# Dilated units later in the pipeline, a rope in pairs of rows, and wide value matmuls in a two-layer encoder

## Chip, cores, metric

The kernel runs on one core of one Trainium2 chip. The metric is the device time of one execution in microseconds. Five engines work side by side: TensorE (PE, with its weight loads shown as PEld), VectorE (DVE), ScalarE (ACT), GpSimd (POOL) and SyncE (SP, which issues DMAs). Each works off its own list of instructions in order, and they wait for one another by semaphores.

## What is computed

A two-layer encoder on 256 tokens of width 1024, in float32. Each layer projects the normalised input to three attention mixers and to gates, adds the gated mixers, and ends with a SwiGLU block:

```
for l in range(DEPTH):
    h = rms_norm(x, g_mix[l]); proj = h @ w_in[l]
    c_q, c_kv, k_r, qkv_b, qkv_c, gate_logits = split(proj)
    y_a = mla_mixer(c_q, c_kv, k_r, ...)                       # 8 heads
    q_b = apply_rope(qkv_b[:, :, 0], cos_b, sin_b)             # 12 heads of 64
    k_b = apply_rope(qkv_b[:, :, 1], cos_b, sin_b)
    y_b = dilated_mixer(q_b, k_b, qkv_b[:, :, 2])              # 3 dilations x 4 heads
    y_c = neighbourhood_mixer(*qkv_c, rpb[l])                  # 8 heads
    gates = sigmoid(gate_logits)
    x = x + (gates[0]*(y_a @ w_pa) + gates[1]*(y_b @ w_pb) + gates[2]*(y_c @ w_pc)) @ w_o[l]
    h = rms_norm(x, g_ffn[l])
    x = x + (silu(h @ w1[l]) * (h @ w3[l])) @ w2[l]
```

`apply_rope` splits a head's 64 rows into two halves x1 and x2 and returns x1 cos - x2 sin and x2 cos + x1 sin, so that row i needs row i + 32 of its head.

## The kernel before

**Split products.** Every large product is made of three matmuls in a rounded type (fp32r): weights and activations are each split into a high and a low part, and high x high, high x low and low x high are added in PSUM (`mm3`, and `v_mm` where the tokens are stationary and the weights move). Weights come as chunks of 128 x 1024 float32 in a fixed order (`PLAN`, made by `plan`), by DMAs on SP's queue into `raw` (6 buffers). ACT casts a chunk to `hi` (L292) and DVE subtracts to `lo` (L294), 4 buffers each. `take` hands out the next chunk and has the one after it split. `pack_weights` lays the chunks out on the host.

**Units.** Attention is cut into units of one half of the queries: 8 of kind c (neighbourhood, a head pair each), 8 of kind a (latent, a head pair each), 8 of kind b (dilated, one head of each of the three groups). A unit passes a pipeline of slots: in a slot's end the newest unit gets its scores (PE), the one before it is transposed (PE, `ps_t`) and copied (ACT), and the one before that is multiplied with V (PE, `ps_y`). In a slot's begin DVE normalises p (L510, L513) ahead of the transposes. `add_units` puts units into the list `todo`; each `slot_end` takes one. Slots stand in the code between the weight tiles: 6 around the dilated q tiles, 6 around the dilated values, 6 around the dilated k tiles, then one behind each of the 24 gate tiles. The units of kind c and a fill the first 16 slots and leave the pipeline in the next two, so the units of kind b, added behind the last k tile, enter with gate tile 0.

**Rope.** `b_tiles` makes the 6 q (or k) tiles in 3 pairs. Behind a pair ACT copies the PSUM bank to t0 (L858), four DMAs on ACT's own queue (L860) exchange blocks of 32 partitions into t1, and DVE multiplies the bank with the cosines into t2 (L861). `rope_end`, called in the middle of the next pair and behind the last, has POOL multiply t1 with the sines (L834) and add (L836 to QB or KB, L839 for the first pair, which then goes through `stack` with two DMAs on POOL's queue). t0, t1, t2 and other scratch share one tag, `t2k`, with 4 buffers in rotation. A dilated unit's scores are two 256-column products with Q0 and K0 and, for each of the other two dilations, two 64x64 products with QB and KB (each shown as two PE records): the first dilation's take the middle pair of tiles, the second's the last pair.

**Values.** Three value tiles of 256 columns (`v_tile`), each with two chunks of 512 weight rows, 48 matmuls, into one PSUM bank of tag g (2 banks in rotation, shared with the q, k and gate tiles). Behind each stand two slots. Tile 0 is evicted by two ACT operations (L696), tile 1 by four on 64 partitions (L880), tile 2 by two and two DMAs (L885).

**What sets the order.** The code gives priorities, and a scheduler that simulates the engines while the kernel is built puts each engine's instructions in a fixed order: an instruction is placed when its inputs are ready in that simulation. So PE's list has matmuls of the next tile in between a unit's steps.

The lines that the change touches are `consts`, `plan`, `pack_weights`, and in `encoder` L859 (DMAs of the rope), L870 to L887 (values), L892 (`add_units` of kind b) and L903 to L905 (the gate loop).

Of the kernel before, what the change touches and what calls it, by code (L numbers as in the profile page):

```python
# [10 lines left out]
F32 = mybir.dt.float32  # L11
# [12 lines left out]
EPS = 1e-6  # L24
BIG = 1e30
HD = 64
OFF_B = 416
OFF_C = OFF_B + 3 * 12 * HD
OFF_G = OFF_C + 3 * 8 * HD
# [8 lines left out]
def consts():  # L38


    def rope(dim):
        pos = np.arange(S, dtype=np.float32)
        inv = np.power(np.float32(10000.0), -np.arange(0, dim, 2, dtype=np.float32) / np.float32(dim))
        ang = pos[:, None] * inv[None, :].astype(np.float32)
        return np.cos(ang).astype(np.float32), np.sin(ang).astype(np.float32)

    f = np.float32
    parts = {}
    rows = np.arange(P)
    parts["ident"] = np.eye(P, dtype=f)  # L50
    parts["ones"] = np.ones((P, P), f)
    parts["col"] = np.tile(np.array([1 / 1024, 1 / 256, 1 / 128, EPS], f), (P, 1))
    c, s = rope(32)
    r = np.arange(32)
    cs = c[TOK][:, r % 16].T
    sn = (s[TOK][:, r % 16] * np.where(r < 16, -1.0, 1.0)[None, :]).T
    sc = f(MLA_SCALE)
    for name, v in (("ck", cs), ("sk", sn)):
        parts[name] = v.T.reshape(2, P, 32).transpose(1, 0, 2).reshape(P, 64)

    parts["tm"] = np.concatenate([np.tile(v, (4, 1)) * sc for v in (cs, np.roll(sn, 16, 0))], 1)
    t = TOK


    dm = np.zeros((P, 2, 384), f)
    for h in range(2):
        q = t[h * P : (h + 1) * P][:, None]
        k = t[None, :]
        dm[:, h, 0:256] = np.where(np.abs(q - k) <= 64, 0, -8 * BIG)
        for e in range(2):  # L70
            r = slice(64 * e, 64 * e + 64)
            dm[r, h, 320 - 64 * e : 384 - 64 * e] = np.where((q[r] - q[r].T) % 16 == 0, 0, -8 * BIG)
    c, s = rope(HD)
    d = rows % 64
    parts["cosb"] = c[TOK][:, d % 32].T
    parts["sinb"] = (s[TOK][:, d % 32] * np.where(d < 32, -1.0, 1.0)[None, :]).T
    parts["dmask"] = dm.reshape(P, -1)
    at, col = {}, 0
    for k, v in parts.items():
        at[k] = (col, v.shape[1])  # L80
        col += v.shape[1]
    return np.ascontiguousarray(np.concatenate(list(parts.values()), 1).astype(f)), at
# [12 lines left out]
def plan():  # L95

    out = [(("a", k), 640) for k in range(KC)]
    out += [(("ck", i), 1024) for i in (2, 3)] + [(("cq", i), 1024) for i in range(4)]
    out += [(("uq", 0), 768)] + [(("cv", 0, h), 1024) for h in range(2)] + [(("uq", 1), 768)]
    for k, n in LAST:  # L100
        out += [(("cvk", k, n), 288 * n)] + [(("ukv",), 1024)] * (k == 0)
    out += [(("b", "q", i), 1024) for i in range(6)]
    out += [(("bv", i, h), 1024) for i in range(3) for h in range(2)]
    out += [(("b", "k", i), 1024) for i in range(6)]
    out += [(("g", j, br), 1024) for j in range(8) for br in range(3)]
    for j in range(10):
        if j < 8:
            out += [(("mab", j), 768), (("mc", j), 512)]
        if j > 1:
            out += [(("o", j - 2), 1024)]  # L110
    out += [(("f", c), 1024) for c in range(4)]
    for f in range(2, NF):
        out += [(("w1", f), 1024), (("w3", f), 1024)]
        if f > 2:
            out += [(("w2", f - 3), 1024)]
    out += [(("w2", f), 1024) for f in range(NF - 3, NF)]
    return out
# [6 lines left out]
def pack_weights(i, l):  # L124
# [17 lines left out]
    def part(key):  # L142
        n = key[0]
        if n == "a":
            c = np.concatenate([np.arange(384), nb_heads("ck", 0), nb_heads("ck", 1)])
            return w_in[P * key[1] : P * key[1] + P, c]
        if n in ("ck", "cq"):
            return tiles(w_in, nb_heads(n, key[1]))
        if n == "cvk":
            c = np.concatenate([OFF_C + 1280 + np.arange(256), 384 + n32])  # L150
            return tiles(w_in[P * key[1] : P * (key[1] + key[2])], c)
        if n in ("cv", "bv"):
            base = OFF_C + 1024 if n == "cv" else OFF_B + 1536
            return tiles(w_in[512 * key[2] : 512 * key[2] + 512], base + 256 * key[1] + np.arange(256))
        if n == "uq":

            cols = [h * 96 + n64 for h in range(4 * key[1], 4 * key[1] + 4)]
            cols += [h * 96 + 64 + n32 for h in range(key[1], 8, 2)]
            return tiles(w_uq, np.concatenate(cols))
        if n == "ukv":  # L160
            ks = np.concatenate([h * P + n64 for h in range(8)])
            return tiles(w_ukv, np.concatenate([ks, ks + 64]))
        if n == "b":
            base = OFF_B + (0 if key[1] == "q" else 768)
            t = key[2]
            return tiles(w_in, heads(base, (2 * t, 2 * t + 1)))
        if n == "g":
            return tiles(w_in, OFF_G + key[2] * D + key[1] * P + np.arange(P))
        cols = np.arange(key[1] * P, key[1] * P + P)
        if n == "mab":  # L170
            return np.concatenate([tiles(i["w_pa"][l], cols), tiles(i["w_pb"][l], cols)], 1)
        if n == "mc":
            return tiles(i["w_pc"][l], cols)
        if n == "o":
            return i["w_o"][l][cols]
        if n == "w2":
            return i["w2"][l][cols]
        if n == "f":
            k = slice(256 * key[1], 256 * key[1] + 256)
            return np.concatenate(  # L180
                [
                    np.concatenate([i[w][l][k][c * P : c * P + P, f * P : f * P + P] for f in (0, 1) for w in ("w1", "w3")], 1)
                    for c in range(2)
                ],
                1,
            )
        return tiles(i[n][l], cols)
# [45 lines left out]
def encoder(ctx: ExitStack, tc: tile.TileContext, x, w, gains, cst, rpb, gfin, out):  # L233
# [375 lines left out]
    if True:  # L609
# [33 lines left out]
        for l in range(NL):  # L643
# [201 lines left out]
            def b_tiles(w_, dst):  # L845
                for i2 in range(3):
                    o = bank("g", "ps_g")
                    for i in range(2):
                        slot_begin()
                        n_tile(l, o[:, cols(i, S)], ("b", w_, 2 * i2 + i))  # L850
                        if i == 0:
                            rope_end()
                        if i == 1:
                            o3 = o.rearrange("p (n s) -> p n s", n=2)
                            t0 = tmp.tile([P, 512], F32, tag="t2k", name="t0", bufs=4)
                            t1 = tmp.tile([P, 512], F32, tag="t2k", name="t1", bufs=4)
                            t2 = tmp.tile([P, 2, S], F32, tag="t2k", name="t2", bufs=4)
                            act.copy(t0, o)  # L858
                            for q in range(4):  # L859
                                act.dma_start(t1[cols(q, 32)], t0[cols(q ^ 1, 32)])  # L860
                            dve.tensor_mul(t2, o3, bc(CR, 2))  # L861
                        slot_end()
                    rope.append((t1.rearrange("p (n s) -> p n s", n=2), t2, dst, w_, i2))
# [3 lines left out]
            K0 = tmp.tile([P, 2, 4, S], F32R, tag="ks", name="K0", bufs=1)  # L867
            KL = [K0[:, e, 2:4, :] for e in range(2)]
            other_rows(KL)
            for i in range(3):  # L870
                o = bank("g", "ps_g")
                slot_begin()
                v_tile(o, "bv", i)
                rope_end()
                if i == 0:
                    v_out(VB, o, 0, RT)
                elif i == 1:
                    for b in range(4):
                        r, t = cols(b % 2, 64), b // 2
                        act.activation(VB[r, 2 + b, :], o[r, cols(t, S)], AF.Copy, scale=RT[r, t : t + 1])  # L880
                else:
                    v2 = tmp.tile([P, 2, 256], F32, tag="t2k", name="v2", bufs=4)
                    v_out(v2, o, 0, RT)
                    for b in range(2):
                        act.dma_start(VB[cols(1 - b, 64), 2 + b :: 2, :], v2[cols(b, 64)])  # L885
                slot_end()
                slot_begin()  # L887
                slot_end()
            KB = tmp.tile([P, 4, S], F32, tag="kb", name="KB", bufs=1)
            b_tiles("k", KB)  # L890
            rope_end()
            add_units(  # L892
                "b", 4, Q=QB, K=KB, V=VB, V12=VB[:, 2:6, :], Q0=[Q0[:, e] for e in range(2)], K0=[K0[:, e] for e in range(2)], L=KL
            )


            GL0 = tmp.tile([P, 16, S], F32, tag="big", name="GL0", bufs=1)
            GL1 = [tmp.tile([P, 4, S], F32, tag=t, name="GL1", bufs=b) for t, b in (("u4a", 2), ("u4a", 2), ("v4", 1))]
# [4 lines left out]
            for i2 in range(12):  # L903
                o = bank("g", "ps_g")
                for i in range(2):  # L905
                    slot_begin()
                    n = 2 * i2 + i
                    n_tile(l, o[:, cols(i, S)], ("g", n // 3, n % 3))
                    if i == 1:
                        (d0, n0), (d1, n1) = logits(n - 1), logits(n)  # L910
# [210 lines left out]
```

## Time and profile before

| | us |
|---|---|
| median of 3 runs (923.6 to 926.31) | 926.07 |
| the profiled execution | 925.92 |
| its span, first to last instruction | 924.1 |
| PE busy | 906.0 |
| DVE busy | 660.8 |
| ACT busy | 519.1 |
| POOL busy | 128.9 |

The granted TensorE clock was 0.997 of full speed over the span. Busy time of PE is a sum over modelled ends: a 256-column matmul is shown with 0.28 us though the next one starts 0.12 later, so the starts tell the pace and a gap between starts tells a wait. A wait's idle time, in square brackets in a row, counts from the shown end.

The stretch that the change touches runs, in layer 0, from about 62 us (first dilated q tile) over 81 (values) and 109 (k tiles) to about 205 (last gate tile), and in layer 1 some 453 us later.

### The profile page before, as it was taken

The page shows a single profiled execution, that of the slowest core. Times are in us where ns is not written, and L with a number is a line of the kernel's source. Part 1 is how long each engine was busy: PE and PEld are TensorE (multiplying, and loading weights), DVE is VectorE, ACT ScalarE, POOL GpSimd, SP SyncE. Part 2 cuts the span into 40 slices and gives each one's busy share as a digit, 9 for nine tenths or more (in the row PEclk, how much of TensorE's full clock was granted, in tenths as well). Part 3 has the DMA queues.
Part 4 walks back from the last instruction along what each step waited for, and adds up shares of the span by engine and source line. Part 5 has one row for each costly group of instructions (what it writes and reads, how often), then busy time and mean ns, then how long its engine had stood idle before and what let it go on. Part 6 is the DMA issues. An engine that isn't in the chain of part 4 may idle for free. (4 is left out here: it accounts for less than half of the span.)

```text
span 924.1 us, 18598 instructions
## 1 busy us (share of the span) xinstructions
PE 906.0 (98%) x7446; PEld 871.0 (94%) x7446; DVE 660.8 (72%) x1003; ACT 519.1 (56%) x858; POOL 128.9 (14%) x138
## 2 busy tenths in 40 slices
PE   8999999999999999999999999999999999999996
PEld 6999898999999999999999989899999999999995
DVE  6987877555888766666699888665577976666663
ACT  6776875533566544444477778655355654444443
POOL 2223112000022100000023240400000210000000
PEclk9999999999999999999999999999999999999998
DMA  8985455344675766655467644533457566555531
GB/s 290 286 289 174 133 149 150 107 153 148 193 223 183 258 209 195 184 185 184 119 237 213 211 147 135 173 117 124 145 178 214 168 212 205 184 193 184 195 124 45
DMA packets 53414, 166.71 MB, mean 180 GB/s; under 512 B 6736, under 2 KB 7504, under 8 KB 53328
## 3 DMA queue, kind: packets, MB, share of 16 engines
q1 hardware_dynamic: 48384, 158.69, 53.7%
q0 software_dynamic: 1920, 3.15, 1.6%
q10 hardware_dynamic: 3024, 3.69, 1.5%
q8 instruction: 58, 0.95, 0.4%
q14 instruction: 28, 0.23, 0.1%
HBM read 157.64 MB, written 1.05 MB: 172 GB/s over the span
## 5 line engine op out<-in xcount | busy, mean ns | idle before, releaser
L294 DVE TENSOR_TENSOR lo<-raw,hi 128x1024 fp32r<-128x1024 f32 (+4 forms) x306 | 373.3, 1227 | 153.4 <-ACT hi L292 152.1
L292 ACT CAST hi<-raw 128x1024 fp32r<-128x1024 f32 (+5 forms) x308 | 304.1, 992 | 301.8 <-PE ps_g L318 162.7
L318 PE MATMUL ps_g<-XH,hi 128*128 128x256 f32 x1392 | 390.0, 281 | 1.2 <-ACT hi L292 1.2
L318 PE MATMUL ps_g<-XH,lo 128*128 128x256 f32 x1392 | 387.9, 281 | 1.6 <-DVE lo L294 1.6
L318 PE MATMUL ps_g<-XL,hi 128*128 128x256 f32 x1392 | 389.3, 280 | 0.0
L318 PEld LDWEIGHTS ps_g<-XH,hi 128*128 128x128 f32 x1392 | 261.5, 188 | 5.2 <-issue 1.9
L318 PEld LDWEIGHTS ps_g<-XH,lo 128*128 128x128 f32 x1392 | 260.2, 188 | 5.3 <-issue 2.7
L318 PEld LDWEIGHTS ps_g<-XL,hi 128*128 128x128 f32 x1392 | 261.7, 188 | 1.6 <-issue 0.3
L318 PE MATMUL ps_acc<-HL,hi 128*128 128x256 f32 x608 | 109.3, 279 | 0.0
L318 PEld LDWEIGHTS ps_acc<-HL,hi 128*128 128x128 f32 x608 | 93.1, 188 | 0.0
L318 PE MATMUL ps_acc<-HL,lo 128*128 128x256 f32 x304 | 84.2, 280 | 0.0
L995 POOL TENSOR_TENSOR SG<-fab 128x256 f32<-128x256 f32 x44 | 34.5, 786 | 305.7 <-DVE fab L991 302.5
L318 PEld LDWEIGHTS ps_acc<-HL,lo 128*128 128x128 f32 x304 | 57.1, 188 | 0.0
L318 PE MATMUL ps_acc<-hi,HL 128*128 128x512 f32 x176 | 55.3, 395 | 0.0
L318 PE MATMUL ps_g<-hi,XL 128*128 128x256 f32 (+1 forms) x160 | 45.9, 287 | 0.0
L318 PE MATMUL ps_g<-hi,XH 128*128 128x256 f32 (+1 forms) x160 | 45.4, 284 | 0.0
L318 PE MATMUL ps_g<-lo,XH 128*128 128x256 f32 (+1 forms) x160 | 45.2, 285 | 0.0
L991 DVE TENSOR_TENSOR fab<-ps_g,RB 128x512 f32<-128x512 f32 x40 | 27.6, 691 | 21.9 <-PE ps_g L318 21.9
L528 ACT COPY pT<-ps_t 128x512 f32<-128x512 f32 (+1 forms) x48 | 26.0, 551 | 29.0 <-PE ps_t L518 21.8
L318 PEld LDWEIGHTS ps_acc<-hi,HL 128*128 128x128 f32 x176 | 31.7, 188 | 6.1
L318 PE MATMUL ps_acc<-lo,HL 128*128 128x512 f32 x88 | 34.8, 395 | 0.0
L834 POOL TENSOR_TENSOR t<-t,CSR 128x512 f32<-128x512 f32 x12 | 19.7, 1644 | 107.9 <-DMA t<-t 79.1
(194 smaller groups left out, 1263.0 us busy)
## 6 DMA issues: line engine op xcount, KB each, us to landing
raw<-in_w SPq DMA_DIRECT2D x250, 512.0 KB, 3.6
raw<-in_w SPq DMA_DIRECT2D x20, 384.0 KB, 3.1
raw<-in_w SPq DMA_DIRECT2D x16, 320.0 KB, 3.1
braw<-in_rpb SPq DMA_DIRECT2D x16, 256.0 KB, 5.2
raw<-in_w SPq DMA_DIRECT2D x16, 256.0 KB, 2.7
t<-t ACTq DMA_DIRECT2D x48, 64.0 KB, 4.4
raw<-in_w SPq DMA_DIRECT2D x4, 432.0 KB, 4.9
KCt<-KCt POOLq DMA_DIRECT2D x8, 128.0 KB, 5.8
```

What stands on the lines that cost most here:

```text
L292: act.copy(hi[:, :width], t[:, :width])
L294: ins = eng.tensor_sub(lo[:, :width], t[:, :width], f32(hi[:, :width])).ins
L318: pe.matmul(o, a, b, start=start, stop=stop, skip_group_check=True)
L528: act.copy(u.pT[:, :n], u.tr[:, :n])
L834: pool.tensor_mul(t13, t13, bc(SR, 2))
L991: dve.tensor_mul(ab, o.rearrange("p (n s) -> p n s", n=2), bc(RB, 2))
L995: pool.tensor_mul(s[:, 1, :], ab[:, 0, :], ab[:, 1, :])
```

## The change

Three things are edited together.

1. The rows of each dilated q and k head are laid out so that row i and its partner i + 32 are neighbours (`PAIRS`, in the weights' columns and in the sine and cosine tables). The exchange is then even rows with odd rows: two DMAs of 64 partitions, with a step of two, for four of 32.
2. Value tiles 0 and 1 are made together, with moving operands of 512 weight columns: four chunks of 256 weight rows x 512 columns, each for both token halves, into two banks `o2` of tag g at once, one slot behind each chunk. In the last chunk the matmuls are sorted by token half. All six evictions stand behind the fourth chunk. Value tile 2 is as before, with its slot and an empty one; the number of slots stays 6.
3. `add_units` of kind b moves from behind the last k tile to the gate loop, ahead of the slot of gate tile 3.

```
+PAIRS = np.arange(HD).reshape(2, 32).T.reshape(-1)
...
-    d = rows % 64
+    d = PAIRS[rows % 64]
...
-    out += [(("bv", i, h), 1024) for i in range(3) for h in range(2)]
+    out += [(("bv", 0, q), 1024) for q in range(4)] + [(("bv", 2, h), 1024) for h in range(2)]
...
+        if n == "bv" and key[1] == 0:
+            return tiles(w_in[256 * key[2] : 256 * key[2] + 256], OFF_B + 1536 + np.arange(512))
...
-            return tiles(w_in, heads(base, (2 * t, 2 * t + 1)))
+            return tiles(w_in, np.concatenate([base + h * HD + PAIRS for h in (2 * t, 2 * t + 1)]))
...
-                            for q in range(4):
-                                act.dma_start(t1[cols(q, 32)], t0[cols(q ^ 1, 32)])
+                            for q in range(2):
+                                act.dma_start(t1[q::2], t0[1 - q :: 2])
...
-            for i in range(3):
-                o = bank("g", "ps_g")
+            o2 = [bank("g", "ps_g") for _ in range(2)]
+            for q in range(4):
                 slot_begin()
-                v_tile(o, "bv", i)
-                rope_end()
...
+                wt = take(l, "bv", 0, q)
+                order = [(kk, t) for kk in range(2) for t in range(2)]
+                for kk, t in order if q < 3 else sorted(order, key=lambda v: v[1]):
+                    v_mm(o2[t], wt, cols(kk, 512), 2 * q + kk, t, q + kk == 0)
+                if q == 0:
+                    rope_end()
+                if q == 3:
+                    for t in range(2):
+                        act.activation(VB[:, t, :], o2[t][:, :256], AF.Copy, scale=RT[:, t : t + 1])
+                        for b in range(2 * t, 2 * t + 2):
+                            r = cols(b % 2, 64)
+                            act.activation(VB[r, 2 + b, :], o2[t][r, 256:], AF.Copy, scale=RT[r, t : t + 1])
                 slot_end()
...
             KB = tmp.tile([P, 4, S], F32, tag="kb", name="KB", bufs=1)
             b_tiles("k", KB)
             rope_end()
-            add_units(
-                "b", 4, Q=QB, K=KB, V=VB, V12=VB[:, 2:6, :], Q0=[Q0[:, e] for e in range(2)], K0=[K0[:, e] for e in range(2)], L=KL
-            )
...
             for i2 in range(12):
                 o = bank("g", "ps_g")
                 for i in range(2):
+                    n = 2 * i2 + i
+                    if n == 3:
+                        add_units(
+                            "b", 4, Q=QB, K=KB, V=VB, V12=VB[:, 2:6, :], Q0=[Q0[:, e] for e in range(2)],
+                            K0=[K0[:, e] for e in range(2)], L=KL,
+                        )
                     slot_begin()
-                    n = 2 * i2 + i
```

## Rows read from the trace of the kernel before

**Rows 1.** The page's busy time by engine (us, share of the span, instructions): TensorE.

```profile
PE 906.0 (98%) x7446; PEld 871.0 (94%) x7446; DVE 660.8 (72%) x1003; ACT 519.1 (56%) x858; POOL 128.9 (14%) x138
```

**Rows 2.** The list of PE's own waits over the whole run: who waited for whom, us in total, times, longest.

```profile
PE ps_s L318 <- POOL KB L836: 2.6, 2, 1.5
...
PE ps_t L518 <- DVE p L513: 1.3, 3, 0.6
```

**Rows 3.** The timeline of PE in layer 0 around the first dilated unit: start us, duration us, engine, line, operation, count, and in brackets the idle time before it with its releaser.

```profile
141.77 0.28 PE L318 MATMUL ps_g<-XH,hi 128*128 128x256 f32 x1
143.58 0.33 PE L318 MATMUL ps_s<-KB,QB 64*64 64x64 f32 x4 [1.53 <-POOL KB L836]
143.84 0.39 PE L318 MATMUL ps_g<-XL,hi 128*128 128x256 f32 x1
144.06 0.28 PE L318 MATMUL ps_g<-XH,lo 128*128 128x256 f32 x1
```

**Rows 4.** The same place in layer 1.

```profile
594.47 0.28 PE L318 MATMUL ps_g<-XH,hi 128*128 128x256 f32 x1
595.80 0.33 PE L318 MATMUL ps_s<-KB,QB 64*64 64x64 f32 x4 [1.06 <-POOL KB L836]
```

**Rows 5.** The timeline of POOL in layer 0 for the middle and the last k pair.

```profile
140.01 1.30 POOL L834 TENSOR_TENSOR t<-t,CSR 128x512 f32<-128x512 f32 x1 [5.76 <-DVE lo L294]
141.40 2.13 POOL L836 TENSOR_TENSOR KB<-t,t 128x512 f32<-128x512 f32 x1
...
148.94 1.31 POOL L836 TENSOR_TENSOR KB<-t,t 128x512 f32<-128x512 f32 x1
```

**Rows 6.** The timeline of PE in layer 0: the third visit of dilated scores, and the last matmul of gate tile 3.

```profile
151.82 0.34 PE L318 MATMUL ps_s<-KB,QB 64*64 64x64 f32 x8
...
154.54 0.28 PE L318 MATMUL ps_g<-XH,lo 128*128 128x256 f32 x1
```

**Rows 7.** The timeline of PE in layer 0 between value tiles 0 and 1, where two units' steps follow one another.

```profile
92.94 0.36 PE L318 MATMUL ps_s<-KCt,QC 128*128 128x256 f32 x1
93.47 0.44 PE L518 MATMUL ps_t<-C,p 128*128 128x128 f32 x2 [0.16 <-DVE p L513]
...
93.98 0.28 PE L318 MATMUL ps_s<-YL,QC 128*128 128x256 f32 x1
94.81 0.70 PE L518 MATMUL ps_t<-C,p 128*128 128x128 f32 x4 [0.56 <-DVE p L513]
```

**Rows 8.** The same place in layer 1.

```profile
546.65 0.28 PE L318 MATMUL ps_s<-YL,QC 128*128 128x256 f32 x1
547.50 0.70 PE L518 MATMUL ps_t<-C,p 128*128 128x128 f32 x4 [0.57 <-DVE p L513]
```

**Rows 9.** The timeline of DVE in layer 0 in the stretch of the values, and its cosine product of the last q pair in layer 1.

```profile
82.41 2.36 DVE L294 TENSOR_TENSOR lo<-raw,hi 128x1024 fp32r<-128x1024 f32 x2
87.31 0.69 DVE L861 TENSOR_TENSOR t<-ps_g,CSR 128x512 f32<-128x512 f32 x1 [2.54 <-POOL QB L836]
...
91.73 1.68 DVE L513 TENSOR_SCALAR p<-p,m 128x256 f32<-128x256 f32 x2
...
539.99 0.69 DVE L861 TENSOR_TENSOR t<-ps_g,CSR 128x512 f32<-128x512 f32 x1 [1.18 <-POOL QB L836]
```

**Rows 10.** The timeline of POOL in layer 0 for the middle q pair.

```profile
83.58 2.33 POOL L834 TENSOR_TENSOR t<-t,CSR 128x512 f32<-128x512 f32 x1 [4.39 <-DMA t<-t]
85.99 1.28 POOL L836 TENSOR_TENSOR QB<-t,t 128x512 f32<-128x512 f32 x1
```

**Rows 11.** The timeline of ACT and its queue (ACTq) in layer 0: DMA issues of the middle q pair, the first of the last q pair, and the evictions of value tile 0.

```profile
76.51 1.18 ACTq L860 DMA_DIRECT2D t<-t  x2
...
79.09 1.21 ACTq L860 DMA_DIRECT2D t<-t  x1
...
87.30 0.52 ACTq L860 DMA_DIRECT2D t<-t  x1
...
94.28 0.83 ACT L696 ACTIVATE VB<-ps_g,RT 128x256 f32<-128x256 f32 x2
```

**Rows 12.** By source line, the rope's DMAs (issue duration in ns, minimum, median, maximum, then first and last start) with their time to landing, and the value DMAs; and by DMA issue, the value DMAs (count, KB each, median us from issue to landing).

```profile
L860 ACTq DMA_DIRECT2D t<-t x48: 514/594/1226, 68.7 to 595.0; - x48
...
DMA to landing us min/median/max: 1.9/4.4/5.9
...
L885 ACTq DMA_DIRECT2D VB<-v x4: 632/656/707, 112.9 to 566.3; - x4
...
VB<-v ACTq DMA_DIRECT2D x4, 128.0 KB, 3.5
```

**Rows 13.** The timeline of PE in layer 0 in value tile 0: its first matmul, its fourth, its thirteenth and its last.

```profile
81.46 0.28 PE L318 MATMUL ps_g<-hi,XH 128*128 128x256 f32 x1
...
81.81 0.28 PE L318 MATMUL ps_g<-hi,XH 128*128 128x256 f32 x1
...
85.91 0.28 PE L318 MATMUL ps_g<-hi,XH 128*128 128x256 f32 x1
...
90.05 0.28 PE L318 MATMUL ps_g<-lo,XH 128*128 128x256 f32 x1
```

**Rows 14.** The timeline of PE in the SwiGLU block of layer 1, where 512 weight columns move: the first of three matmuls, and the first of the next three.

```profile
813.33 0.63 PE L318 MATMUL ps_acc<-hi,HL 128*128 128x512 f32 x2
...
814.03 0.63 PE L318 MATMUL ps_acc<-hi,HL 128*128 128x512 f32 x2
```

More of the change, by code (lines that the diff above doesn't have):

```diff
@@ L869, in encoder @@
             other_rows(KL)
-            for i in range(3):
-                o = bank("g", "ps_g")
+            o2 = [bank("g", "ps_g") for _ in range(2)]
+            for q in range(4):
                 slot_begin()
-                v_tile(o, "bv", i)
-                rope_end()
[L875 to L885, printed above, removed]
-                slot_end()
-                slot_begin()
-                slot_end()
+                wt = take(l, "bv", 0, q)
[10 more added lines that the diff above has]
+                            act.activation(VB[r, 2 + b, :], o2[t][r, 256:], AF.Copy, scale=RT[r, t : t + 1])
+                slot_end()
+            o = bank("g", "ps_g")
+            slot_begin()
+            v_tile(o, "bv", 2)
+            v2 = tmp.tile([P, 2, 256], F32, tag="t2k", name="v2", bufs=4)
+            v_out(v2, o, 0, RT)
+            for b in range(2):
+                act.dma_start(VB[cols(1 - b, 64), 2 + b :: 2, :], v2[cols(b, 64)])
+            slot_end()
+            slot_begin()
+            slot_end()
             KB = tmp.tile([P, 4, S], F32, tag="kb", name="KB", bufs=1)
```

## Prediction

> **What bounds the kernel now.** I read the page's busy line first: TensorE (PE) has work in 906.0 of 924.1 us [rows 1] (the span stands in the table of the profile). So only two kinds of saving count: fewer or cheaper matmul columns, and PE's own waits. The second view is the list of PE's waits over the run [rows 2]: 2.6 us for KB in two waits, which is one in each of the two layers, and 1.3 us for the transposes that wait for the normalised p of a unit. Work taken from ScalarE (ACT), VectorE (DVE) or GpSimd (POOL) is worth only what it does to such waits. The profiled execution took 925.92 us with a span of 924.1; the median of the three runs shown is 926.07, so I sum against 925.92 and read it as the median, 0.15 us apart.
>
> The third view, PE's order of time around the first wait, shows what it is. At 141.77 one gate matmul starts; the next PE instruction, the first 64x64 score matmul of dilated unit 0, starts at 143.58 and is released by the KB addition on POOL [rows 3]. Layer 1 shows the same from 594.47 to 595.80 [rows 4]. POOL shows why: the rope product of the middle k pair starts at 140.01 and the KB addition at 141.40 takes 2.13 us, to 143.53 [rows 5]. The last k pair is added at 148.94, until 150.25; the scores that need it are a third visit, at 151.82 [rows 6]. So the units are added when two thirds of their K are not there. TensorE works in a fixed order, so what stands behind the wait stands still.
>
> The transposes of the second wait stand in the stretch of the dilated values: 92.94 to 93.47 and 93.98 to 94.81 in layer 0 [rows 7], 546.65 to 547.50 in layer 1 [rows 8]. They wait for p, whose scaling starts on DVE only at 91.73 and takes 1.68 us for two [rows 9]. DVE had stood 2.54 us before 87.31, waiting for POOL's QB addition to give back a shared scratch buffer (tag t2k, 4 buffers), and 1.18 us in layer 1 [rows 9, 10].
>
> **Part 1, units three gate tiles later.** Nothing is added or removed; eight units with their drain move from gate tiles 0 to 9 to tiles 3 to 12 of 24. Unit 0 is now asked for after gate tile 3, whose last matmul started at 154.54 before [rows 6]; without the wait (about 1.7) and without the visits of units 0 and 1 in between (some 0.6) that is about 152.2 on the old clock. KB was whole at 150.25 [rows 5], so 2 us of cover are left even if the rope gets no faster; were it gone, each us of lateness would cost one again. Start to start the two gaps are 1.81 and 1.33; an unwaited matmul is 0.12 behind its forerunner [rows 13], so the wait costs 1.53 to 1.69 and 1.06 to 1.21. I take 1.6 and 1.1: **minus 2.7**. Units 0 and 1 now need two visits for three. Leaving a 64x64 visit costs 0.22 at the first gate matmul behind it (143.84 to 144.06 [rows 3]) where 0.12 is usual, entering one about the same: **minus 0.4** for both layers (0 to 0.6). The drain has 11 gate tiles behind it, so the end of the stage costs nothing.
>
> **Part 2, rope in pairs.** 12 pair tiles issued 4 DMAs each, 48 of 64 KB, median issue 594 ns on ACT's queue, 4.4 us to land; now 2 of 128 KB. No row has one with a partition step of two; the nearest is the value DMA over 64 partitions, 128 KB: 656 ns, 3.5 us [rows 12]. So a pair costs 1.3 us of ACT's queue for 2.4; bounds are 514 to 1226 ns an issue and 1.9 to 5.9 us to land, the extremes of the 64 KB rows. PE waits for neither directly. What it moves is the chain of the middle q pair: its issues ran from 76.51 to 80.30, because the fourth stood behind ACT work that itself waited [rows 11], and POOL's product started at 83.58 [rows 10]. With two issues the last is out near 77.7; 3.5 us on, POOL can start near 81.3 to 81.5, some 2 us earlier. QB then ends near 85 and not 87.27, and DVE's 2.54 and 1.18 us waits shrink to about nothing. On POOL and SP's queue no instruction is moved past another.
>
> **Part 3, 512 columns.** Per layer 96 matmuls of 256 columns become 48 of 512, with the same weight bytes, casts and evictions. Three 256-column matmuls take 0.35 (81.46 to 81.81), 117 ns each [rows 13]; three of 512 columns take 0.70 (813.33 to 814.03), 233 [rows 14]. 96 x 0.117 = 11.23; 48 x 0.231 to 0.233 = 11.09 to 11.18: 0.05 to 0.14 a layer; **minus 0.3** at most for both layers, and I take 0.3. The Trainium skill, TensorE: Matmul & The Clock Gate, section Back-to-back issue gap, has two figures: one gives a 512-column matmul about 216 ns alone, the other about 131 ns sustained in a stream with weight loads. This trace has weight loads throughout and 233, so it speaks against the second; what that would bring is the last rival.
>
> The slots now lie one behind each of four chunks where two stood together behind 48 matmuls. Between two units' transposes stand 12 wide matmuls, 2.8 us, and DVE comes to p earlier by Part 2. The transposes' gaps, less 0.12 each, are 0.41 + 0.71 + 0.73: **minus 1.9** (bounds 0 and 1.9; the end, since both of its causes are touched).
>
> The price lies in PSUM. Tag g has two banks, and both are now held from the first chunk to the fourth. The second is the bank of the last q pair, free when DVE's product at 87.31 has ended, at 88.00 [rows 9]. Before, its next user came at 90.18, behind a whole value tile. Now it is wanted as soon as PE has done the first chunk's matmuls for the other half: values begin at 81.46, and by 85.91 PE had done twelve value matmuls, 1.4 us, and 3.05 us of two units' work [rows 13]; six wide ones take the same 1.4. With the chain 2 us faster the bank is free near 85.7. If nothing got faster PE would stand 88.0 - 85.9 = 2.1 us, in layer 1 as much (the product ends at 540.68 [rows 9]; the same place on PE is 452.7 later, by [rows 7, 8], 538.6). Bounds 0 and 4.2; **plus 0.8**, nearer the low end.
>
> At this point a rule speaks against the change. The row: POOL's product beside DVE's weight splits took 2.33 us, alone 1.3 [rows 5, 10]. The Trainium skill, SBUF — State Buffer, section Who interferes with whom, says that a DVE instruction with two SBUF inputs and a GpSimd one that reads SBUF exclude each other for a whole instruction. By it a product ready at 81.5 might wait for both splits (82.41 to 84.77), the bank would be free near 86.8, and the 0.8 would be about 2: total 922.6. Trace and rule agree on the direction; I stay with 0.8 because the product would start before the splits.
>
> **Sum.** 925.92 - 2.7 - 0.4 - 0.3 - 1.9 + 0.8 = 921.4 us.
>
> **Rivals.** (a) The wait moves. The first bank wait costs its full 4.2, the rest holds: 925.92 - 5.3 + 4.2 = 924.8; or the transposes wait as before, 921.4 + 1.9 = 923.3. For it: the order of PE is fixed when the kernel is built, and in [rows 3] it left POOL 1.5 us too little. Against: the faster chain. Centre 924.3.
>
> (b) Slower: PE has no bank to run ahead into at either end of the four chunks. At the start the full 4.2. At the end value tile 2 needs the first bank, which waits for three evictions of some 0.47 on ACT. Evictions of a value tile began 3.95 us behind its last matmul (90.33 to 94.28) [rows 11, 13]; 3.95 + 1.4 less the cover of 1.4 (six wide matmuls) and 1.5 (one unit's work, half of the 3.05) leaves 2.45 a layer. Gains of Part 1 and 3 stay, 3.4, those of the transposes go: 925.92 - 3.4 + 4.2 + 4.9 = 931.6. It turns slower when both bank waits pass 1.7 us a layer together. Against: ACT ran late because its queue stood behind DMA issues that waited for QB (87.30, just behind 87.27) [rows 10, 11], and these come earlier.
>
> (c) The pairs don't land well: a step of two takes the slow ends (1.2 us an issue, 5.9 us to land). Then the chain is as late as before and the case is (a) or (b), counted there.
>
> (d) 512 columns at 131 ns: 96 x (0.231 - 0.131) = 9.6 more, 911.8.
>
> **How the numbers follow.** Forecast 0.63, own range 919.5 to 923.2; (a) 0.26; (b) 0.09; (d) 0.02. A measurement of this kernel can tell about 0.3%, 2.8 us, from no change, so faster means under 923.3. The forecast falls on that side for the most part (0.60 of its 0.63), with (d) and a little of (a): faster 0.63; same 0.28; slower 0.09. For 8 in 10 the range leaves out (d), most of (b) and the low tail: 919.3 to 925.2.
>
> **What would show it.** Part 1: no PE wait for KB, and two runs of eight 64x64 matmuls for units 0 and 1. Part 2: 24 issues, the middle q pair's QB done near 85, DVE's product behind it with no wait. Part 3: 96 value matmuls of 512 columns near 0.23 apart. The price: a wait of ps_g on PE for DVE's product or ACT's copy at the first or the fifth value chunk; over 2 us there in a layer makes the prediction wrong. So would a new wait at the first dilated score.

## The result and the profile after

The changed kernel takes 919.51 us (median of 5 runs, 919.16 to 920.12); the kernel before, run on the same chip, 923.7 (5 runs, 922.92 to 926.31). The ratio over all runs is 0.9947, 95% interval 0.9929 to 0.9965 (the two medians alone would give 0.9955): faster, by more than the 0.3% that the prediction took as what a measurement can tell. The forecast was 921.4, so the direction was right and the time came out 1.9 us lower. Against the 4.5 us that the forecast took off the profiled execution, the medians lie 4.2 us apart and the two profiled executions 6.4. The profiled execution of after takes 919.51 us, its span is 917.7.

The page's busy time by engine, after; it answers to [rows 1]:

```profile
PE 903.4 (98%) x7350; PEld 864.8 (94%) x7350; DVE 660.2 (72%) x1003; ACT 520.2 (57%) x858; POOL 127.4 (14%) x138
```

There are 96 fewer PE instructions because 192 value matmuls of 256 columns have become 96 of 512. The list of PE's own waits, after; it answers to [rows 2]:

```profile
PE ps_f L322 <- DVE XL L399: 2.0, 2, 1.0
PE ps_g L322 <- DVE lo L298: 1.6, 3, 0.5
PE warm L322 <- DVE warm L617: 1.2, 1, 1.2
PE ps_g L322 <- ACT hi L296: 1.1, 1, 1.1
```

No KB and no `ps_t` is left in it. POOL's timeline in layer 0 shows the rope's chain: the middle q pair, then the middle and the last k pair (to be laid beside [rows 10] and [rows 5]):

```profile
79.02 1.31 POOL L838 TENSOR_TENSOR t<-t,CSR 128x512 f32<-128x512 f32 x1 [1.44 <-DMA t<-t]
80.41 1.30 POOL L840 TENSOR_TENSOR QB<-t,t 128x512 f32<-128x512 f32 x1
...
139.57 2.15 POOL L840 TENSOR_TENSOR KB<-t,t 128x512 f32<-128x512 f32 x1
...
143.57 2.18 POOL L840 TENSOR_TENSOR KB<-t,t 128x512 f32<-128x512 f32 x1
```

The middle QB is done at 81.71, where before it was done at 87.27 [rows 10]: 5.6 us earlier, not the 2 of the forecast. ACT's queue and DVE around it, and the rope's DMAs by source line (issue in ns, minimum, median, maximum), answering to [rows 11, 9, 12]:

```profile
76.14 1.12 ACTq L864 DMA_DIRECT2D t<-t  x2
```

```profile
85.29 0.69 DVE L865 TENSOR_TENSOR t<-ps_g,CSR 128x512 f32<-128x512 f32 x1
```

```profile
L864 ACTq DMA_DIRECT2D t<-t x24: 472/508/790, 69.1 to 589.2; - x24
...
DMA to landing us min/median/max: 1.9/3.2/5.7
```

Both issues go out in one piece, 1.12 us, and DVE's cosine product has no bracket behind it: the 2.54 us in which it waited for QB are gone. PE's timeline at the first dilated score in layer 0 shows no wait and eight 64x64 products at once, because the last KB (done at 145.75) is there too:

```profile
150.08 0.29 PE L322 MATMUL ps_g<-XH,lo 128*128 128x256 f32 x1
150.20 0.40 PE L322 MATMUL ps_s<-K,Q 128*128 128x256 f32 x2
150.53 0.45 PE L322 MATMUL ps_s<-KB,QB 64*64 64x64 f32 x8
```

PE's timeline in the dilated values of layer 0: three wide matmuls, then the far end of the four chunks, up to the first matmul of value tile 2:

```profile
84.26 0.39 PE L322 MATMUL ps_g<-lo,XH 128*128 128x512 f32 x1
84.49 0.40 PE L322 MATMUL ps_g<-hi,XH 128*128 128x512 f32 x1
84.72 0.39 PE L322 MATMUL ps_g<-hi,XL 128*128 128x512 f32 x1
...
98.92 0.40 PE L322 MATMUL ps_g<-lo,XH 128*128 128x512 f32 x1
99.24 1.08 PE L322 MATMUL ps_y<-pT,VC 128*64 128x256 f32 x8
100.26 0.66 PE L522 MATMUL ps_t<-C,p 128*128 128x128 f32 x4
100.67 0.96 PE L322 MATMUL ps_s<-AH 128*128 128x256 f32 x6
101.47 0.38 PE L522 MATMUL ps_t<-C,p 128*128 128x128 f32 x2
101.60 0.96 PE L322 MATMUL ps_s<-AH 128*128 128x256 f32 x6
102.40 0.38 PE L522 MATMUL ps_t<-C,p 128*128 128x128 f32 x2
102.53 0.36 PE L322 MATMUL ps_g<-hi,XH 128*128 128x256 f32 x1
```

The pitch is 0.23 (84.26 to 84.72 is two of them). Value tile 2 has to wait for a bank that ACT empties until 102.21, and PE has units' work of 3.3 us to do meanwhile (99.24 to 102.53), so it doesn't stand idle.

**Where the time went.** I counted PE from start to start between two fixed matmuls of each layer, one ahead of the dilated q tiles and one in the last gate tile (39.6 to 207.2 us in layer 0 before). The stretch takes 167.53 and 166.83 before, 163.67 and 163.72 after: 6.97 us less for both layers. Of it 4.59 are the waits that the forecast named (start-to-start gaps of 1.60, 0.41 and 0.72 in layer 0, 1.13 and 0.73 in layer 1). The rest of the run took 0.58 more, 0.43 of it ahead of the stretch of layer 0, so that the profiled executions differ by 6.4 (925.92 to 919.51). That is more than the 4.2 of the medians: before's profiled execution lies near the upper end of its 922.92 to 926.31.

### The profile page after: what moved, and what is told of

It is laid out like the page before. It is cut to its first block, busy times and chain, and to the rows that moved or that the text cites. A ratio compares the mean times of both kernels' runs of the same rounds, so it can differ in the third digit from the quotient of the medians.

```text
span 917.7 us, 18370 instructions
## 1 busy us (share of the span) xinstructions
PE 903.4 (98%) x7350; PEld 864.8 (94%) x7350; DVE 660.2 (72%) x1003; ACT 520.2 (57%) x858; POOL 127.4 (14%) x138
## 4 chain that ended last, share of the span: by engine, by line
PE 93%; DVE 4%; ACT 1%; DMA 1%; issue 0%; SPq 0%; DVEq 0%
PE ps_g L322 63%; PE ps_acc L322 16%; PE ps_s L322 3%; PE ps_y L322 3%; PE ps_t L522 2%; PE ps_c L322 2%; DVE lo L298 2%; PE ps_f L322 1%; PE ps_a L322 1%; DVE XL L399 1%; DMA X<-in_x 1%; ACT hi L296 1%; DVE t L975 0%; DVE X L987 0%; PE ps_r L322 0%
## 5 line engine op out<-in xcount | busy, mean ns | idle before, releaser
L322 PE MATMUL ps_g<-hi,XH 128*128 128x256 f32 (+2 forms) x128 | 40.4, 316 | 0.0
L322 PE MATMUL ps_g<-hi,XL 128*128 128x256 f32 (+2 forms) x128 | 40.0, 313 | 0.0
L322 PE MATMUL ps_g<-lo,XH 128*128 128x256 f32 (+2 forms) x128 | 39.9, 315 | 0.0
L926 DVE TENSOR_TENSOR GL<-ps_g,RB 128x512 f32<-128x512 f32 x20 | 13.8, 692 | 24.0 <-PE ps_g L322 24.0
```

Of the source, the lines that this page charges most:

```text
L322: pe.matmul(o, a, b, start=start, stop=stop, skip_group_check=True)
L926: dve.tensor_mul(d0[:, n0 : n0 + 2, :], o.rearrange("p (n s) -> p n s", n=2), bc(RB, 2))
```

## Experiments

The theory on record: Part 1 takes away the wait for KB, Parts 2 and 3 those of the transposes, and the faster rope spares PE the wait for a second bank. The rivals were that the parts don't add up and one of them brings everything; that Part 2 acts by its row layout, or by the number of issues on ACT's queue alone; and that what helps is the other order of the instructions which the build chooses for another number of DMAs, not a faster chain.

**The kernel before, again.** No edit.

> The kernel before, unchanged, profiled once more. Theory L (the profiled execution of before, 925.92 us, stood at the upper end of what that kernel does): a second profile has a span of 921 to 922 us, near 923.5 us in time, and shows where the 2 to 3 us more of the first one stood. Theory W (waits are the whole gain): the two PE waits for KB (2.6 us) and the three for transposes (1.3 us) stand in it again within 0.3 us, wherever the rest lies. Time against before: ratio 1.000.

Measured: 925.0 against 924.57, ratio 1.000 (0.9987 to 1.0013). The KB waits (2.0 us) and the transposes' waits (1.4) are there in this execution too. It took 926.31, so theory L, a shorter execution, missed. What the change removes isn't an accident of the profile shown.

**One part alone.** Three kernels, each the kernel before with one of these edits (Part 2 with `PAIRS` in the tables and in the weights' columns):

```
e1_units
-            add_units("b", ...)                # behind the last k tile
...
+                    if n == 3:
+                        add_units("b", ...)
```

```
e2_pairs
-                            for q in range(4):
-                                act.dma_start(t1[cols(q, 32)], t0[cols(q ^ 1, 32)])
+                            for q in range(2):
+                                act.dma_start(t1[q::2], t0[1 - q :: 2])
```

```
e3_wide
-                v_tile(o, "bv", i)
...
+                    v_mm(o2[t], wt, cols(kk, 512), 2 * q + kk, t, q + kk == 0)
```

> Only Part 1: dilated units enter with gate tile 3; rope and values as before. Theory W: both KB waits go (2.7 us by starts) with one visit of scores fewer a layer, the transposes' waits of the value stretch stay: 3 to 4 us below before. Rival (the wait moves): a wait of PE at the first dilated score behind gate tile 3, or nothing gained: within 1 us of before.

> Only Part 2: the rope's exchange by two DMAs of 64 partitions. Theory W: no PE wait is touched directly; the middle q pair's QB ends 2 us earlier (near 85 in layer 0), DVE's waits for it shrink, the transposes' waits (1.9 us by starts) shrink by half or more and the KB waits from 1.6 and 1.1 to under 1: 1 to 2.5 us below before. Rival (the pairs land late because of the step of two): no row of POOL's chain earlier, time within 0.5 us of before.

> Only Part 3: two value tiles of 512 columns in two banks. Theory W: columns and joints give 0.5 to 1 us and the transposes' waits go (1.9 us), KB waits stay: 2 to 3 us below before. Rival B (both g banks held): without the faster rope PE waits at the second bank for DVE's cosine product, 1 to 2 us a layer, and the time is within 1 us of before or above it.

| kernel | median us | ratio (95%) |
|---|---|---|
| units alone | 920.87 | 0.9954 (0.9938 to 0.9970) |
| pairs alone | 920.41 | 0.9942 (0.9922 to 0.9961) |
| wide alone | 925.69 | 1.0011 (0.9997 to 1.0024) |

(against 924.57). Units alone and pairs alone each bring nearly the whole gain; the wide values alone bring none. The list of PE's waits says why. Units alone, the one row of a unit's steps that is left:

```profile
PE ps_t L518 <- DVE p L513: 0.7, 2, 0.4
```

Pairs alone, the whole list:

```profile
PE ps_f L320 <- DVE XL L397: 1.7, 2, 0.9
PE ps_g L320 <- DVE lo L296: 1.6, 3, 0.5
PE ps_g L320 <- ACT hi L294: 1.5, 2, 0.9
PE warm L320 <- DVE warm L615: 1.2, 1, 1.2
```

Wide alone:

```profile
PE ps_t L520 <- DVE p L515: 4.0, 3, 1.9
...
PE ps_s L320 <- POOL KB L838: 0.8, 2, 0.6
```

Both of the first two take away the wait for KB, one by asking later, the other by having KB earlier and, as the count below shows, by asking somewhat later too; only the pairs take away the transposes' waits as well. Wide alone makes those waits worse, 4.0 us for 1.3 [rows 2]; the wait at the second bank, which rival B of that run expected, didn't come.

**Two parts together**, by the same edits, and the whole change once more.

> Parts 2 and 3, units entering with gate tile 0 as before. What the earlier runs leave: pairs alone 0.994 with no PE wait left in the stretch, wide alone 1.001 with a wait of the transposes and of KB. Theory W2 (the faster rope carries the gain; wide columns add their 0.26 us a layer once the bank comes free early): 0.993 to 0.994. Rival B (two banks held costs something even with the faster rope): 0.995 to 0.998, with a wait at a first or fifth value chunk.

> Parts 1 and 3, rope by four DMAs. Theory W2: the KB waits go, the transposes' waits that wide values alone showed (4.0 us idle in three) stay or grow: 0.996 to 0.999. Rival (parts add up: units alone 0.9954, wide alone 1.001): 0.9965 as well; the trace tells them apart by whether p or KB ends a wait.

> Parts 1 and 2, values in three tiles of 256 columns. Theory W2: pairs alone already took the KB waits and the transposes' waits, so units add only one visit of scores less a layer, some 0.3 us: 0.9935 to 0.9945. Rival (the two parts add up, 0.9954 x 0.9942): 0.990.

> The whole change once more, beside the other two, to have it on one chip with them: 0.994 by its first comparison (0.9947) and by pairs alone (0.9942). If wide columns and later units add what their pace shows (some 1 us together over pairs alone), 0.993.

| kernel | median us | ratio (95%) |
|---|---|---|
| pairs and wide | 919.86 | 0.9942 (0.9929 to 0.9954) |
| units and wide | 923.28 | 0.9980 (0.9971 to 0.9989) |
| units and pairs | 919.88 | 0.9941 (0.9927 to 0.9954) |
| all three | 919.14 | 0.9936 (0.9921 to 0.9952) |

(against 925.39). With the pairs it hardly matters which other part is there: 0.9936 to 0.9942. Without them the wide values give back half of what the units bring (0.9980 against 0.9954). The place is the far end of the four chunks; PE's timeline of units and wide, layer 0:

```profile
98.61 0.40 PE L320 MATMUL ps_g<-lo,XH 128*128 128x512 f32 x1
98.94 1.08 PE L320 MATMUL ps_y<-pT,VC 128*64 128x256 f32 x8
101.89 0.63 PE L520 MATMUL ps_t<-C,p 128*128 128x128 f32 x4 [1.87 <-DVE p L515]
102.41 0.39 PE L320 MATMUL ps_g<-hi,XH 128*128 128x256 f32 x1
```

PE has `ps_y` to do and then stands for a unit's p, for 1.87 us by the row, and in layer 1 for 1.86. No value matmul can run ahead: both banks of tag g are full until ACT has emptied the first (102.36). It is the far end of rival (b), which has a price of 2.45 a layer in the prediction; the row names p as what ended the wait, but with the bank full until 102.36 an earlier p alone would have started value tile 2 no more than 0.05 sooner. It came only where the rope is slow. In after, the two groups of six `ps_s<-AH` matmuls stand at this place.

**Why the pairs help: layout, number, queue or order?** Four kernels. First the paired rows with four DMAs:

```
e7_pairs_four (on top of the pairs alone)
-                            for q in range(2):
-                                act.dma_start(t1[q::2], t0[1 - q :: 2])
+                            for q in range(4):
+                                h, e = 64 * (q // 2), q % 2
+                                act.dma_start(t1[h + e : h + 64 : 2], t0[h + 1 - e : h + 64 : 2])
```

> Part 2 with its row layout, but four DMAs of 32 partitions with a step of two, in place of two of 64. Theory N (the number of issues on ACT's queue is what made the rope late): the middle q pair's QB ends near 87 as before and the time is within 0.2% of before. Rival S (the step of two, which spreads a DMA over all partitions, lands sooner): QB near 82 as with two DMAs and 0.994 to 0.996.

Measured: 924.8, ratio 0.9995 (0.9985 to 1.0005). PE, DVE, ACT and POOL have the same instructions in the same order as the kernel before, and the waits are back:

```profile
PE ps_s L320 <- POOL KB L838: 2.1, 2, 1.1
...
PE ps_t L520 <- DVE p L515: 0.9, 2, 0.6
```

So the layout and the step of two do nothing by themselves; what helps comes with two instructions for four, and that is two things: fewer issues, and another order of the engines' lists, which differ from before's from 71.5 us on (ACT's first). Next, the kernel before with every second DMA issued on SP's queue, and with eight smaller ones on ACT's:

```
e8_two_queues
-                                act.dma_start(t1[cols(q, 32)], t0[cols(q ^ 1, 32)])
+                                (act, sp)[q % 2].dma_start(t1[cols(q, 32)], t0[cols(q ^ 1, 32)])
```

```
e9_eight
-                            for q in range(4):
-                                act.dma_start(t1[cols(q, 32)], t0[cols(q ^ 1, 32)])
+                            for q in range(8):
+                                act.dma_start(t1[cols(q, 16)], t0[cols(q ^ 2, 16)])
```

> The kernel before with its four exchange DMAs of 32 partitions, but the second and the fourth issued on SP's queue in place of ACT's. Theory N (what makes the rope late is the third and fourth issue on ACT's queue, behind ACT's own work): the middle q pair's QB ends near 82 to 84, the waits for KB and for the transposes fall by half or more, 0.994 to 0.997. Rival T (the number of DMAs itself, each with its own landing, makes it late, on whatever queue): QB near 87, 0.999 to 1.001. SP's queue also carries the weights, in order; a wait for t0 there could hold them back, which would show as PE waits for hi or lo.

> The kernel before with eight exchange DMAs of 16 partitions on ACT's queue, the same bytes: the suspected cost doubled. Theory N: four more issues of some 0.55 us a pair, the middle q pair's QB ends 2 to 4 us later than 87, PE's waits for KB and for transposes grow, 1.004 to 1.012. Rival (issues cost nothing that lasts; two against four was a matter of the layout or of the order): within 0.2% of before.

Measured: two queues 922.18, 0.9969 (0.9957 to 0.9981); eight DMAs 924.01, 0.9978 (0.9967 to 0.9989), both against 925.39. So the number of issues on ACT's queue isn't the cause by itself: with twice as many the kernel is a little faster, not slower as theory N had it. Both runs have another order too (PE's lists differ from before's from 78 us on). POOL's timeline for the middle q pair and the middle k pair, two queues:

```profile
86.22 1.28 POOL L836 TENSOR_TENSOR QB<-t,t 128x512 f32<-128x512 f32 x1
...
135.95 1.30 POOL L836 TENSOR_TENSOR KB<-t,t 128x512 f32<-128x512 f32 x1
```

KB comes at 137.25 and its wait is gone; QB, at 87.50, is as late as before, and 1.2 us of transposes' waits stay. ACT's timeline says why QB is late: before, then two queues, then pairs alone:

```profile
79.08 0.59 ACT L528 COPY pT<-ps_t 128x512 f32<-128x512 f32 x1 [0.73 <-PE ps_t L518]
79.09 1.21 ACTq L860 DMA_DIRECT2D t<-t  x1
```

```profile
79.22 0.51 ACT L340 ACTIVATE p<-p,m 128x256 f32<-128x256 f32 x1 [2.02 <-DVE m L479]
79.23 0.52 ACTq L860 DMA_DIRECT2D t<-t  x1
```

```profile
75.73 0.58 ACT L860 COPY t<-ps_g 128x512 f32<-128x512 f32 x1
76.33 1.12 ACTq L862 DMA_DIRECT2D t<-t  x2
77.97 0.59 ACT L530 COPY pT<-ps_t 128x512 f32<-128x512 f32 x1 [1.66 <-PE ps_t L520]
```

With two issues on ACT's queue as with four, the last one goes out 0.01 us behind an ACT operation that had itself waited, for PE or for DVE. In pairs alone both stand in ACT's list directly behind the copy to t0, ahead of a copy that waits 1.66 us. For QB it is the place of the last issue in ACT's list that counts, more than the number. With eight DMAs QB is later still, and its lateness shows as another wait, for the bank that DVE's cosine product frees; POOL, then PE's list:

```profile
88.51 2.15 POOL L836 TENSOR_TENSOR QB<-t,t 128x512 f32<-128x512 f32 x1
```

```profile
PE ps_g L318 <- DVE t L861: 2.3, 2, 1.4
```

Last, a longer chain in the order of the pairs alone: each DMA cut into pieces. All four pieces are read from the same quarter, so the exchange is left out.

```
e11_cut (on top of the pairs alone)
-                                act.dma_start(t1[q::2], t0[1 - q :: 2])
+                                act.dma_start(t1[q::2].rearrange("p (a b) -> p a b", a=4), bc(t0[1 - q :: 2, 0:128], 4))
```

> The pairs alone, but each of the two DMAs is cut into pieces: 64 partitions x 4 pieces of 512 B for 64 x 2 KB, all four pieces read from the first quarter of t0, so that what arrives in t1 is not the exchange. The list of every engine stays the same as in the pairs alone, operation by operation; only the duration of the rope's chain can differ. The pairs alone have 920.41 (0.9942), QB done at 81.99 with 3.6 us to spare before DVE's cosine product at 85.58, and the middle KB done at 142.10 with 0.47 us to spare before the scores at 142.57. Theory C (the lateness of the chain decides): with x us more of chain, the wait for KB comes back as x - 0.47 a layer while x is under 3.6 for QB, and the transposes' waits come back only above that; with x of 2 the time is 920.4 + 2 x 1.5 = 923.5 (ratio near 0.998). Theory O (the fixed order of the lists decides, the duration of the chain hardly): no wait beyond 0.5 comes back, 920 to 921 (0.994 to 0.995), though the landing takes longer. If the pieces cost nothing (issue near 0.57, landing near 3.0), the run tells nothing between the two.

Measured: 921.29 against 925.65, 0.9955 (0.9942 to 0.9969). The pieces cost little: the median issue is 628 ns for 566 in the pairs alone, and the median landing is 3.3 us in both (not the 3.0 that the expectation has for the pairs alone). POOL and PE in layer 0:

```profile
140.73 2.17 POOL L838 TENSOR_TENSOR KB<-t,t 128x512 f32<-128x512 f32 x1
```

```profile
142.55 0.40 PE L320 MATMUL ps_s<-K,Q 128*128 128x256 f32 x2
142.96 0.33 PE L320 MATMUL ps_s<-KB,QB 64*64 64x64 f32 x4
```

KB is done at 142.90, just ahead of the scores, so no wait comes back, and the run alone can't tell theory C from theory O: from the copy to t0 to the end of the addition the middle k pair takes 9.12 us in layer 0, against 9.24 in the pairs alone, so the chain isn't longer there. The following count tells more. For each kernel, from the same fixed matmul of layer 0 as above: when the middle QB and the middle KB are done, when the first scores with KB start (us), and how many weight matmuls PE's list has ahead of them:

| kernel | QB | KB | scores | matmuls ahead |
|---|---|---|---|---|
| before | 47.65 | 103.90 | 103.95 | 577 |
| pairs layout, four DMAs | 47.09 | 102.81 | 102.87 | 577 |
| pairs alone | 41.74 | 101.85 | 102.32 | 576 |
| pairs cut | 41.87 | 102.83 | 102.88 | 576 |
| two queues | 47.57 | 97.32 | 102.23 | 576 |
| eight DMAs | 50.28 | 102.13 | 106.77 | 611 |
| units alone | 47.11 | 102.99 | 111.29 | 648 |
| after | 41.65 | 101.67 | 110.48 | 600 |

(A 512-column matmul counts once, and there are 48 of them for 96, so the 600 of after is the place of the 648 of units alone.) With the units moved the wait for KB ends because the order asks later, by design. With eight DMAs the order asks 35 matmuls later and KB is 1.8 us earlier as well. Before, with pairs alone and with two queues the scores stand behind as many weight matmuls, 576 or 577. With two queues PE's units' steps ahead are the same too, so what ends the wait is that KB is 6.6 us earlier; but the copy that starts its chain runs 3.7 us earlier, in another order. In pairs alone and pairs cut PE's list has eight more `ps_y` matmuls ahead of the scores (64 for 56), about 1 us. What that is worth is seen by laying four DMAs beside pairs cut: KB is done at the same time, 102.81 and 102.83, and yet PE stood 1.02 us for it with four DMAs and not at all with the cut ones (each had stood some 0.5 us for something else further ahead). So in the pairs alone the wait for KB ends by both, KB 2.05 us earlier in layer 0 (4.70 in layer 1) and PE's own work ahead about 1 us longer; the runs don't part the two further. The margin is small in layer 0: 0.47 us, 0.05 in `e11_cut` (in layer 1, pairs alone, 3.92).

For the transposes the time of QB decides, and four runs show it without a change of order: before, before again, four DMAs and units alone have the same lists on PE, DVE, ACT and POOL up to 141 us. Their middle QB of layer 0 is done at 47.65, 47.82, 47.08 and 47.11 on the clock of the table, and the transposes' gaps of that layer, less 0.12 each, sum to 1.12, 1.27, 0.50 and 0.55 us: a microsecond for a microsecond. The pairs bring QB 5.9 us earlier by that clock, though its chain starts only 0.2 us earlier (the copy to t0 at 35.48 for 35.70).

So the rival of the other order holds in part. Of the 5.8 us that the pairs alone save between the fixed matmuls, 4.6 are waits and 1.2 are not; the place of the issues in ACT's list and PE's longer work ahead of KB are the build's choice as well. What the two DMAs would save in before's order no run shows.

## Why the prediction was right and which step failed

- **Part 1, minus 2.7: right.** The KB waits measured 1.60 and 1.13; they are gone, and the middle KB has 8.8 and 9.2 us to spare, the last one 4.8 and 3.6. Units alone shows it, with the two runs of eight 64x64 products.
- **Joints, minus 0.4: too small.** Beyond the waits and the columns the stretch lost another 2.2 us (6.97 - 4.59 - 0.2). I had priced only the visits of two units. These microseconds belong to the order of PE's list: before, before again and four DMAs, which share one order, take 329.8 us for both layers less their waits, within 0.03 of one another; the whole change takes 327.4, in its second run 327.5, and pairs alone 328.6. One part shows: PE's visits to matmuls smaller than 128x128 (64x64, and the 128x64 of `ps_y`) fall from 46 to 42 (44 in pairs alone). A visit costs about 0.2, since the first small one starts 0.21 behind a full one for the usual 0.12 and the second full one behind the visit 0.22 [rows 3]; four fewer are 0.8 by this estimate. What the rest is made of stays open.
- **Part 2, nothing for PE directly: the step that failed.** The sum has no term for the pairs themselves; they were to bring QB 2 us forward and so to help the transposes and the second bank. Alone they take 5.8 us from the two stretches, more than the 4.5 of the whole forecast: all the waits, 4.6, and 1.2 beyond them. The working moved the middle q pair's product from 83.58 to 81.3 to 81.5; it came at 79.02. The last of two issues was forecast near 77.7 and was out at 77.26, and the data landed 1.6 us behind that, not 3.5. POOL's product was also short, 1.31 for 2.33. The working also held that no instruction is moved past another on POOL's queue; the build did move some, on POOL too: the last q pair's product starts at 87.14, ahead of a DMA issue (91.34) that stood ahead of it before (90.84 and 91.93). And I had not asked what the same two DMAs do to the k pairs: alone they take away the KB wait that I had credited to Part 1. The two parts buy the same 2.7 us; whichever comes second gets almost nothing for it.
- **Columns, minus 0.3: about 0.2.** Uninterrupted wide matmuls have a median pitch of 0.232, two of 256 columns 0.234: 48 x 0.002 is about 0.1 a layer, within the 0.05 to 0.14. Wide alone is 1.001. Rival (d) fell: no run shows 131 ns.
- **Transposes, minus 1.9: right in size, wrong in cause.** The gaps of 0.41, 0.72 and 0.73 are gone. The pairs do that, alone; the slots between wide chunks, which I had named as the other cause, make the transposes' waits longer when the rope is slow (4.0 us in wide alone, 3.7 in units and wide).
- **Second bank, plus 0.8: it didn't come.** QB's 5.6 us make DVE's product end at 85.98, and PE had units' work until 87.71, the start of its next wide matmul. POOL's product at 79.02 met no split of DVE's and took 1.31 us for the 2.33 of before, so nothing was delayed there. The Trainium skill, SBUF — State Buffer, section Who interferes with whom, has a DVE instruction with two SBUF inputs contend with a GpSimd one that reads SBUF. The trace agrees with it elsewhere: KB, with splits beside it, took 2.15 and 2.18.
- **Rivals.** (a) Both halves of it fell. (b) was real at its far end but needs the slow rope; units and wide shows it at 1.87 and 1.86 us in its two layers, and there the kernel is still faster than before. (c) fell: a step of two issues in 508 ns and lands in 3.2 us.

In sum: 4.6 of waits as forecast, 0.8 of a bank wait that wasn't there, and 2.4 for the 0.7 of joints and columns. No run beats the whole change by more than its interval; pairs with either other part come within 0.1%.

## What to carry to other kernels

Price each part of a change alone and then ask which wait it removes: two parts that remove the same wait, one by asking later and one by delivering earlier, don't add up. An edit of a few DMAs can also change the order of every engine's list when a scheduler lays it out, so compare the lists before a time is put down to the DMAs. When a chain of DMAs feeds another engine, look for where an issue is stuck behind other work of its queue; fewer issues that go out in one piece can pull the chain in by far more than their issue time. A layout that widens an operation and holds two buffers at once should be tried together with whatever makes their release earlier, since alone it may only lengthen waits.

## What the runs showed of the hardware

- Two DMAs of 128 KB in a row landed in 3.2 us (median, after), four of 64 KB in 4.4 [rows 12] and eight of 32 KB in 3.3, so the wait isn't a matter of bytes alone. Cutting 2 KB rows into 512 B pieces added 62 ns to an issue and nothing to the median landing (3.3 us with and without).
- A partition step of two cost nothing that shows: for 32 partitions 555 ns an issue and 4.2 us to land with it (four DMAs), 594 ns and 4.4 without (before), all medians.
- POOL's 128x512 operations of the rope took 1.26 to 1.32 us in before and after where no split of DVE's lay beside them, and anything from 1.28 to 2.36 where one did. In after the one that started first kept its time: the QB addition at 80.41 took 1.30, and a split that began at 80.76 took 2.02 for the usual 1.21; a split of 138.96 was under way when the KB addition began at 139.57 and took 2.15.
- On PE a matmul smaller than 128x128 started 0.21 us behind a full 256-column one, where full ones follow one another by 0.12, and the second full one behind such a visit by 0.22 (medians in before and after).
